# Layer A, pairs 1 to 6: the products of probabilities with values in one piece, begun later behind the border of the half products

## The chip, the cores and the metric

One core of one Trainium2 chip runs the whole program. The metric is device time in microseconds (us), the median of the runs shown. Five engines work side by side, each through its own list of instructions in order: TensorE (PE), VectorE (DVE), ScalarE (ACT), GpSimd (POOL) and SyncE (SP, which here only issues transfers).

## What is computed

The reference is an encoder block of two layers over 512 tokens of width 1024, 16 heads of 64. Layer A is dilated attention in three groups that are merged by their denominators; layer B is attention over a neighbourhood on a grid. Cut to layer A, where the change is:

```python
def mixer_a(hn, w_in, w_out, q_gain, k_gain, t5_bias):
    proj = hn @ w_in
    ...
    for g, (window, dilation) in enumerate(DILATED_PAIRS):
        q = rms_norm(qkv[:, :, g, 0], q_gain[g])
        k = rms_norm(qkv[:, :, g, 1], k_gain[g])
        v = qkv[:, :, g, 2]
        ...
    alpha = jax.nn.softmax(jnp.stack(lses), axis=0)
    y = jnp.sum(alpha[..., None] * jnp.stack(outs), axis=0)
    y = y.reshape(b, s, BRANCH_WIDTH).astype(hn.dtype) * jax.nn.silu(gate)
    return y @ w_out
```

## The kernel before, in words

**Precision.** Every float32 operand of a large product is split into a rounded part and a rest (`wh` and `wl` for weights, `hn_h` and `hn_l` for the normalised input), and a product is three matmuls of 512 columns into a bank of PSUM called `acc`. ACT makes `wh` from the loaded weights `wraw`, and DVE or POOL makes `wl`. `splits` hands out these weight tiles in the order of a plan, one tile of 512 columns being a job; there are 6 buffers for `wh`, 5 for `wl`, 8 for `wraw`.

**Layer A.** The 16 heads are worked in 8 pairs, 0 to 7, by `main_a(hc)`. From pair 1 on, the projections to q, k and v are made by seven half-size block products in Strassen's manner (`product`), 32 jobs a pair with the gate and the first value group. The point behind the product that ends the queries is stamped `border`; one half product (4 jobs, 24 matmuls) follows it, and then the next pair begins.

**Side work.** A second generator, `side`, does the attention of pair hc while `main` makes the projections of pair hc + 1. For each pair it runs `attn_a`: the scores in two halves (`scores`, tile `log`), softmax on DVE and ACT (`minima`, `exponents`, `normalise`), a turn of the probabilities `p` into `pt`, transfers `pt<-pt` on SP, the transpose of the values (`v_a`, tile `tp`), the products of probabilities with values (`weigh`, four banks `o`, tile 32*64 for groups 1 and 2 and 128*64 for group 0), the multiplication with the gate on DVE (`weighed`, `gt<-gt,o`), a send of `gt` to memory (`y_d<-gt`), and the transposes of the next pair's queries and keys (`q_a`, `k_a`, tiles `tp<-rawq` and `tp<-rawk`). Those read `rawq` and `rawk` after DVE has scaled them (`rawq<-rawq,rs`, `rawk<-rawk,rs`), the scale coming from a chain of nine small DVE operations that begins at `nv<-ss` (`unit`).

**What sets the order.** The order on PE is the order in which the program is written out. `run` steps `main` one group of matmuls at a time and lets `side` put in a piece when a clock that the program counts itself (`clock`, in ns of PE work as `matmul` estimates it) has reached the time that the piece asked for; a guard in `main` can force `side` on until a stamp is there. `later_on(delay, job)` puts small jobs of DVE and ACT into a list of timers, and `tick` runs those that are due. `weigh` yields twice, so that the 96 products of a pair come in three pieces: 32 for group 1, 32 for group 2, 32 for group 0, with the gaps that the caller names. The order on DVE, ACT, POOL and SP is set by a scheduler from dependencies and the order of issue, but for lines marked to stay in program order.

Of the kernel before, what the change touches and what calls it, by code (L numbers as in the profile page):

```python
# [26 lines left out]
NHC = 8  # L27
# [23 lines left out]
def tile_hybrid_encoder(  # L51
# [287 lines left out]
    clock = [0.0]  # L339
# [22 lines left out]
                hs = slice(64 * hd, 64 * hd + 64)  # L362
                matmul(os[hd], l(hs), r(hs), share=2, start=(n == 0), stop=(last and n == 2))

    timers = []

    def later_on(delay, job):

        timers.append((clock[0] + delay, job))
        timers.sort(key=lambda t: t[0])  # L370

    def tick(all_of=False):
        while timers and (all_of or timers[0][0] <= clock[0]):
            timers.pop(0)[1]()

    chores = []

# [267 lines left out]
    def part(n, cols=512):  # L645
        half = rk[:, 2048 * (n % 2) : 2048 * (n % 2) + 4 * cols]
        return half.rearrange("p (i c) -> p i c", i=4)

    def raw_q():
        return wk.tile([P, 4, 512], F32, tag="rawq", name="rawq", bufs=1)  # L650

    def sums():
        return wk.tile([P, 32], F32, tag="ss", name="ss", bufs=3)
# [75 lines left out]
    def main_a(hc):  # L729
        if hc == 0:  # L730
            yield from project_qk(512, 8, "rawq", hc, None, first=True, need="na")
            yield from project_qk(512, 4, "rawk", hc, ("rs", "a"), after=renorm)
            return

        kv, a, b, c, box = part(hc), [], [], [], [sums(), sums()]

        def new():
            if len(box) == 2:
                box.append(raw_q())
            return box[2]  # L740

        hn = lambda k0, t0: lambda k: (t[:, k0 + k, t0 : t0 + H] for t in (hn_h, hn_l))
        mixed = lambda n: lambda k: (t[:, n, k, :] for t in (mix_h, mix_l))

        def keep(i, acc):
            act.copy(kv[:, 2 + i, :], acc)

        def put11(i, acc):
            act.copy(kv[:, i, :], acc)
            squares_soon(kv[:, i, :256], box[0], i, 4)  # L750

        def put_v(i, acc):
            vec.tensor_sub(new()[:, 2 + i, :], acc, kv[:, 2 + i, :])

        def put_u(i, acc):
            vec.scalar_tensor_tensor(
                box[2][:, i, :], acc, -1.0, kv[:, 2 + i, :], op0=ALU.mult, op1=ALU.subtract
            )

        def put12(i, acc):  # L760
            t = box[2][:, i, :]
            vec.tensor_add(t, t, acc)
            squares_soon(t, box[1], i, 8)

        def put22(i, acc):
            t = box[2][:, 2 + i, :]
            vec.tensor_sub(t, t, acc)
            squares_soon(t, box[1], 2 + i, 8)

        def put21(i, acc):  # L770
            t = kv[:, 2 + i, :]
            vec.tensor_add(t, t, acc)
            squares_soon(t[:, :256], box[0], 2 + i, 4)

        yield from product(a, hn(0, 0), True, keep, ("w", hc - 2))
        yield from gate_a(hc - 1)
        yield from product(a, hn(KH, 0), False, put11)
        if hc > 1:
            yield from v0_a(hc - 1, ("scored", hc - 1))
        for n, acc, first, put in ((0, c, True, put_v), (1, b, True, put_u), (3, c, False, put12), (2, b, False, put22)):  # L780
            yield "mix", n
            yield from product(acc, mixed(n), first, put, ("q", hc - 1) if n == 0 else None)
        normed(box[2], box[1], 8, "rawq", hc)
        if hc == 1:
            yield from v0_a(hc - 1)
        stamp["border", hc] = clock[0]
        yield
        yield from product(b, hn(KH, H), False, put21)
        if hc == NHC - 1:
            st["y_h"] = big.tile([P, KT, S], F32R, tag="yh", name="y_h")  # L790
            st["y_l"] = big.tile([P, KT, S], F32R, tag="yl", name="y_l")
        normed(kv, box[0], 4, "rawk", hc)
        if hc == NHC - 1:
            yield ("back",)
            yield from v0_a(hc)
            yield from gate_a(hc)
# [57 lines left out]
                dl, src, gk[:, g : g + 1], dh.bitcast(F32), op0=ALU.mult, op1=ALU.subtract  # L854
            )

    def side_by_side(mms, outs=1, gaps=None):


        for i, (d, v, r) in enumerate(mms):  # L860
            if i and outs > 1 and i % 16 == 0:
                yield gaps[i // 16 - 1]
            for hd in range(2):
                hs = slice(64 * hd, 64 * hd + 64)
                matmul(d(hs), v(hs), r(hd), share=2 * outs if i < 32 and outs > 1 else 2,
                       start=i < outs, stop=i >= len(mms) - outs)
# [35 lines left out]
    def weighed(hc, os):  # L902
        gt, rest = st.pop(("gate", hc))
        for _ in rest:
            pass
        for j in range(4):
            g = by_class(gt)[:, :, j]
            vec.tensor_mul(g, g, os[j][:, :P].rearrange("p (t r) -> p t r", t=4))
        return gt
# [91 lines left out]
    def attn_a(hc):  # L1001
# [107 lines left out]
            dst = sb(pq, at(t, hd), [[256, 2], [1024, 4], [1, 32]])  # L1109
            vec.tensor_copy(dst, tp.rearrange("p (i a r) -> p i a r", i=2, a=4))  # L1110

        def weigh(first=2200):
            os, v0 = [bank("o") for _ in range(4)], st.pop("v0")
            mms = []
            for g in range(2):
                for b in range(4):
                    for j in range(4):
                        own = slice(32 * j, 32 * j + 32)
                        c, d = P * g, 1024 * b + 256 * (2 + g)
                        mms.append((  # L1120
                            lambda hs, j=j: os[j][hs, :P],
                            lambda hs, own=own, b=b, c=c: v12[own, b, c + hs.start : c + hs.stop],
                            lambda hd, own=own, d=d: pq[own, d + at(0, hd) : d + at(0, hd) + P],
                        ))
            for i in range(4):
                (ta, ia), (tb, ib) = ((i - 1, 1), (i, 0)) if i else ((0, 0), (3, 1))
                n, m = 32 * (tb - ta), 256 * (ib - ia) + 32 * (tb - ta)
                for a in range(4):
                    mms.append((
                        lambda hs, a=a, d=32 * ta, n=n: sb(os[a][hs], d, [[n, 2], [1, 32]]),  # L1130
                        lambda hs, i=i: v0[:, i, hs],
                        lambda hd, d=run * a + 256 * ia + 32 * ta, m=m: sb(t0[0], d + 128 * hd, [[m, 2], [1, 32]]),
                    ))
            yield from side_by_side(mms, 4, (first, 2200))
            return os

        if last:
# [16 lines left out]
            stamp["ya", "last", "p"] = 0  # L1154
            yield from v_a(hc)
            yield "wait", ("gate", hc), 500
            gt = weighed(hc, (yield from weigh()))
            held[0] = False
            stamp["ya", "turned"] = 0
            for c in range(4):  # L1160
# [26 lines left out]
        if hc:  # L1187
            st["e", hc + 1] = bias_a(hc + 1, True)
        if hc:
            yield "wait", ("border", hc + 1), 0  # L1190
        yield "wait", ("gate", hc), 4000
        gt = weighed(hc, (yield from weigh((2200, 6000)[hc] if hc < 2 else 4800 if hc == NHC - 2 else 3300)))
        if not hc:
            st["e", hc + 1] = bias_a(hc + 1)
        if hc < NHC - 2:
# [455 lines left out]
```

## Time and profile before

| | |
|---|---|
| median of 3 runs | 826.37 us (826.36 to 826.44) |
| the profiled execution | 827.79 us, its span 826.0 us |
| mean granted TensorE clock | 0.996 |
| busy: PE, DVE, ACT, POOL | 816.8, 608.3, 520.4, 236.2 us |
| products `o` of layer A, first and last | 117.4 us and 537.1 us into the span |

In the profile a line of the timeline has the start, the duration, the engine, the line of the program (L347 is the helper `matmul`, L351 `transpose`, L87 the wrapper that all other engines' operations go through), the operation, the tile written and the tiles read, the shape, and how many were merged. A bracket behind it has the time that the engine had stood idle, and who ended that. PE's matmuls are pipelined: the distance between starts says what a matmul costs, not its duration. A matmul on plain float32 operands leaves two records, so the 32 products of a group, `x32` in the order, are `x64` in the trace.

### The profile page before, as it was taken

How to read it: one execution, taken by the hardware profiler on the slowest of the kernel's cores; microseconds unless marked ns; L12 is line 12 of the kernel's file. 1: busy time of each engine (PE TensorE's matmuls, PEld its weight loads, DVE VectorE, ACT ScalarE, POOL GpSimd, SP SyncE). 2: the span in 40 equal slices, each digit the busy share in tenths (PEclk: the TensorE clock that was granted, in tenths of full speed). 3: DMA queues.
4: the chain of work that ended last, by engine and by line, in shares of the span. 5: the costliest groups of instructions: out<-in, count | busy, mean ns of one | idle time of the engine just before them, and what ended most of it. 6: DMA issues, size and time to landing. Idle time of an engine off the chain costs nothing.

```text
span 826.0 us, 17436 instructions
## 1 busy us (share of the span) xinstructions
PE 816.8 (99%) x6410; PEld 660.3 (80%) x6410; DVE 608.3 (74%) x1546; ACT 520.4 (63%) x1075; POOL 236.2 (29%) x194
## 2 busy tenths in 40 slices
PE   9999999999999999999999999999999999999998
PEld 7876788778778888888888888888888787888776
DVE  7897896797798777777777785547656769776453
ACT  8668665855755945946946947644567476766340
POOL 0042402442351531531531525412111122122220
PEclk9999899999999999999999999999999999999999
DMA  9426666576575784784774755384244563744122
GB/s 344 149 64 177 158 155 165 116 207 182 119 196 182 163 214 135 162 212 138 162 211 138 162 174 182 97 300 153 94 162 141 152 186 132 206 115 145 36 103 102
DMA packets 54869, 131.92 MB, mean 160 GB/s; under 512 B 6784, under 2 KB 24384, under 8 KB 54656
## 3 DMA queue, kind: packets, MB, share of 16 engines
q1 hardware_dynamic: 48304, 108.27, 41.5%
q0 software_dynamic: 6048, 22.02, 14.8%
q8 instruction: 50, 0.82, 0.4%
q10 hardware_dynamic: 432, 0.52, 0.2%
q14 instruction: 35, 0.29, 0.1%
HBM read 111.73 MB, written 11.72 MB: 149 GB/s over the span
## 4 chain that ended last, share of the span: by engine, by line
PE 94%; DVE 2%; ACT 2%; issue 1%; POOL 1%; DMA 0%; SPq 0%; DVEq 0%; ACTq 0%; POOLq 0%
PE acc L347 78%; PE o L347 6%; PE log L347 6%; PE tp L351 4%; POOL wl L87 1%; ACT wh L87 1%; DVE mixed L87 0%; DMA wraw<-in_w 0%; ACT rawk L87 0%; DVE wl L87 0%; PE pk L347 0%; DVE pt L87 0%; DVE ss L87 0%; DVE mix_l L87 0%; ACT k L87 0%
## 5 line engine op out<-in xcount | busy, mean ns | idle before, releaser
L87 ACT CAST wh<-wraw 128x512 fp32r<-128x512 f32 (+1 forms) x344 | 206.5, 611 | 142.8 <-PE acc L347 120.6
L87 POOL TENSOR_TENSOR wl<-wraw,wh 128x512 fp32r<-128x512 f32 (+1 forms) x126 | 172.5, 1384 | 415.3 <-PE acc L347 170.6
L87 DVE TENSOR_TENSOR wl<-wraw,wh 128x512 fp32r<-128x512 f32 (+1 forms) x218 | 166.9, 769 | 57.5 <-PE acc L347 36.6
L347 PE MATMUL acc<-wh,hn_h 128*128 128x512 f32 x424 | 172.2, 407 | 0.9 <-ACT wh L87 0.6
L347 PE MATMUL acc<-wl,hn_h 128*128 128x512 f32 x424 | 165.3, 391 | 0.4 <-DVE wl L87 0.4
L347 PE MATMUL acc<-wh,hn_l 128*128 128x512 f32 x424 | 165.2, 391 | 0.0
L87 ACT ACTIVATE p<-p,mn 128x256 f32<-128x256 f32 (+2 forms) x248 | 138.1, 582 | 29.9 <-DVE mn L87 29.8
L347 PEld LDWEIGHTS acc<-wh,hn_h 128*128 128x128 f32 x424 | 79.5, 188 | 21.1 <-issue 3.4
L347 PEld LDWEIGHTS acc<-wh,hn_l 128*128 128x128 f32 x424 | 79.6, 188 | 17.4
L347 PEld LDWEIGHTS acc<-wl,hn_h 128*128 128x128 f32 x424 | 79.8, 188 | 15.6 <-DVE wl L87 1.2
L347 PE MATMUL acc<-wh,mix_h 128*128 128x512 f32 x224 | 89.8, 401 | 0.0
L347 PE MATMUL acc<-wl,mix_h 128*128 128x512 f32 x224 | 88.5, 395 | 1.2 <-POOL wl L87 1.2
L347 PE MATMUL acc<-wh,mix_l 128*128 128x512 f32 x224 | 88.0, 393 | 0.0
L347 PE MATMUL acc<-hn_h,wh 128*128 128x512 f32 x192 | 78.5, 409 | 0.0
L347 PE MATMUL acc<-hn_l,wh 128*128 128x512 f32 x192 | 75.1, 391 | 0.0
L347 PE MATMUL acc<-hn_h,wl 128*128 128x512 f32 x192 | 75.0, 391 | 0.0
L87 POOL DMA_DIRECT2D wraw<-in_w x42 | 38.7, 936 | 81.7 <-DVE wl L87 74.2
L87 DVE TENSOR_REDUCE ss<-sq 128x8 f32<-128x512 f32 (+1 forms) x80 | 44.7, 573 | 21.8 <-ACT sq L87 20.9
L87 DVE STREAM_TRANSPOSE pt<-p 128x512 f32<-128x512 f32 (+1 forms) x60 | 40.4, 684 | 21.5 <-ACT p L87 21.5
L347 PE MATMUL acc<-y_h,wh 128*128 128x512 f32 x128 | 51.7, 404 | 0.0
L347 PEld LDWEIGHTS acc<-wl,mix_h 128*128 128x128 f32 x224 | 42.5, 190 | 11.2 <-POOL wl L87 2.0
L347 PEld LDWEIGHTS acc<-wh,mix_h 128*128 128x128 f32 x224 | 42.5, 190 | 10.2 <-issue 1.8
(152 smaller groups left out, 1332.8 us busy)
## 6 DMA issues: line engine op xcount, KB each, us to landing
wraw<-in_w SPq DMA_DIRECT2D x119, 512.0 KB
wraw<-in_w POOLq DMA_DIRECT2D x42, 512.0 KB, 7.4
pt<-pt SPq DMA_DIRECT2D x106, 64.0 KB
td<-tr SPq DMA_DIRECT2D x24, 224.0 KB
pt<-td SPq DMA_DIRECT2D x24, 224.0 KB
e<-l_d SPq DMA_DIRECT2D x32, 112.0 KB
wraw<-in_w SPq DMA_DIRECT2D x6, 384.0 KB
e<-l_d SPq DMA_DIRECT2D x16, 128.0 KB
```

Source lines behind the costliest of these rows:

```text
L87: m = f(*args, **kw)
L347: nc.tensor.matmul(o, l, r, **kw)
L351: nc.tensor.transpose(o, i, ident)
```

## The change

The diff does four things. `weigh` takes both of its gaps from the caller, and a gap of 0 is no yield at all, so in pairs 1 to 6 the 96 products stand in one piece; pairs 0 and 7 keep their gaps of 2200. The wait on the border of the next pair asks for 2300 ns behind it (3800 in pair 6) where it asked for none. A job that a timer issues counts its own timers from the time at which it was due, and no longer from the time at which the list was looked at; this holds for every pair and for layer B. The second tile of sums of squares (`ss`) is taken when the queries' tile is taken, no longer at the pair's start.

```diff
-    timers = []
+    timers, due_at = [], [None]
 
     def later_on(delay, job):
 
-        timers.append((clock[0] + delay, job))
+        timers.append(((clock[0] if due_at[0] is None else due_at[0]) + delay, job))
         timers.sort(key=lambda t: t[0])
 
     def tick(all_of=False):
         while timers and (all_of or timers[0][0] <= clock[0]):
-            timers.pop(0)[1]()
+            due_at[0], job = timers.pop(0)
+            job()
+            due_at[0] = None
...
-        kv, a, b, c, box = part(hc), [], [], [], [sums(), sums()]
+        kv, a, b, c, box = part(hc), [], [], [], [sums()]
 
         def new():
-            if len(box) == 2:
-                box.append(raw_q())
+            if len(box) == 1:
+                box.extend((sums(), raw_q()))
             return box[2]
...
-    def side_by_side(mms, outs=1, gaps=None):
+    def side_by_side(mms, outs=1, gaps=(0, 0)):
 
         for i, (d, v, r) in enumerate(mms):
-            if i and outs > 1 and i % 16 == 0:
+            if i and outs > 1 and i % 16 == 0 and gaps[i // 16 - 1]:
                 yield gaps[i // 16 - 1]
...
-        def weigh(first=2200):
+        def weigh(gaps):
...
-            yield from side_by_side(mms, 4, (first, 2200))
+            yield from side_by_side(mms, 4, gaps)
...
-            gt = weighed(hc, (yield from weigh()))
+            gt = weighed(hc, (yield from weigh((2200, 2200))))
...
         if hc:
-            yield "wait", ("border", hc + 1), 0
+            yield "wait", ("border", hc + 1), 3800 if hc == NHC - 2 else 2300
         yield "wait", ("gate", hc), 4000
-        gt = weighed(hc, (yield from weigh((2200, 6000)[hc] if hc < 2 else 4800 if hc == NHC - 2 else 3300)))
+        gt = weighed(hc, (yield from weigh((0, 0) if hc else (2200, 2200))))
```

The order of instructions shows what moves. On PE, pair 1, the first piece of products stood right at the border, behind the last matmuls on `mix_h` and `mix_l` (the operands of the half products ahead of the border):

```order
L347 MATMUL acc<-wh,mix_h 128x512
L347 MATMUL acc<-wl,mix_h 128x512
L347 MATMUL acc<-wh,mix_l 128x512
L347 MATMUL o<-pt,rawk 64x128 x32
L347 MATMUL acc<-wh,hn_h 128x512
L347 MATMUL acc<-wl,hn_h 128x512
L347 MATMUL acc<-wh,hn_l 128x512
```

In the changed kernel it stands 12 matmuls behind the border, with all three groups in it:

```order
L347 MATMUL acc<-wh,hn_h 128x512
L347 MATMUL acc<-wl,hn_h 128x512
L347 MATMUL acc<-wh,hn_l 128x512
L347 MATMUL o<-pt,rawk 64x128 x64
L347 MATMUL o<-pt_1932,v_1945 64x2x32 x8
L347 MATMUL o<-pt_1932,v_1945 64x64 x24
L347 MATMUL acc<-wh,hn_h 128x512
L347 MATMUL acc<-wl,hn_h 128x512
L347 MATMUL acc<-wh,hn_l 128x512
```

The other two pieces of before are gone from their places, 30 and 12 matmuls further on (18 and 12 in pairs 2 to 5; in pair 6, 24 and none). Behind the piece the first transposes of the next queries come after 30 matmuls (24 in pair 6), where they came 15 behind the third piece (18 in pair 6).

On DVE, pair 3, the next pair's queries were scaled ahead of the multiplication with the gate:

```order
L87 TENSOR_TENSOR rawq<-rawq,rs 128x512
L87 TENSOR_TENSOR wl<-wraw,wh 128x512
L87 TENSOR_TENSOR rawq<-rawq,rs 128x512
L87 TENSOR_TENSOR wl<-wraw,wh 128x512
L87 TENSOR_TENSOR rawk<-rawk,acc 128x512
L87 TENSOR_TENSOR rawq<-rawq,rs 128x512
L87 TENSOR_TENSOR rawk<-rawk,acc 128x512
L87 TENSOR_TENSOR rawq<-rawq,rs 128x512
L87 TENSOR_TENSOR wl<-wraw,wh 128x512
L87 TENSOR_TENSOR gt<-gt,o 128x4x32 x4
```

Now the multiplication, which reads what the piece writes, stands ahead of them, right behind the chain of small operations that gives `rs`:

```order
L87 SCALAR_TENSOR_TENSOR rs<-na,rs 128x32
L87 TENSOR_TENSOR gt<-gt,o 128x4x32 x4
L87 TENSOR_TENSOR rawq<-rawq,rs 128x512 x2
L87 TENSOR_TENSOR wl<-wraw,wh 128x512
L87 TENSOR_TENSOR rawq<-rawq,rs 128x512
L87 TENSOR_TENSOR wl<-wraw,wh 128x512
L87 TENSOR_TENSOR rawk<-rawk,acc 128x512
L87 TENSOR_TENSOR rawq<-rawq,rs 128x512
L87 TENSOR_TENSOR rawk<-rawk,acc 128x512
L87 TENSOR_TENSOR wl<-wraw,wh 128x512
```

So the four scalings of `rawq` changed places with the multiplication, and in DVE's order all that follows, weight rests `wl` among it, stands behind what reads the piece's result.

On ACT, in pair 0, some 60 us into the program, the keys of pair 0 are scaled in sixteen small operations, and `mix_h` is rounded, whose input DVE makes:

```order
L87 ACTIVATE rawk<-rawk,rs 128x64 x4
L87 CAST wh<-wraw 128x512
L87 CAST mix_h<-mixed 128x1024
L87 ACTIVATE rawk<-rawk,rs 128x64 x8
L87 CAST wh<-wraw 128x512
L87 ACTIVATE rawk<-rawk,rs 128x64 x4
L87 ACTIVATE gt<-acc 128x512
```

The timers now count from due times, and the second group of four stands ahead of `mix_h`:

```order
L87 ACTIVATE rawk<-rawk,rs 128x64 x4
L87 CAST wh<-wraw 128x512
L87 ACTIVATE rawk<-rawk,rs 128x64 x4
L87 CAST mix_h<-mixed 128x1024
L87 ACTIVATE rawk<-rawk,rs 128x64 x8
L87 CAST wh<-wraw 128x512
L87 ACTIVATE gt<-acc 128x512
```

One group of four moved from behind the second `wh` to ahead of `mix_h`. On SP the send `y_d<-gt` now stands one load of weights earlier, right behind the bias loads of the next pair; POOL's list is the same in layer A up to two rows in pair 7.

## Prediction

> **What bounds the kernel now.** I read the page first, then who PE waited for, then PE's timeline around the pieces, and last DVE and ACT where the order changes.
>
> ```profile
> PE 816.8 (99%) x6410; PEld 660.3 (80%) x6410; DVE 608.3 (74%) x1546; ACT 520.4 (63%) x1075; POOL 236.2 (29%) x194
> ```
>
> PE is busy for 816.8 of 826.0 us, so only PE's own time and its few waits can be shortened. The longest of those waits:
>
> ```profile
> PE log L347 <- ACT k L87: 1.6, 2, 0.8
> PE acc L347 <- POOL wl L87: 1.2, 2, 0.6
> ```
>
> Each row has the sum in us, the number of times and the longest; the rows left out are smaller or lie ahead of the first product. A gain must come from what the pieces cost PE, from the two waits for POOL, from the two for ACT's `k`, or from the clock.
>
> **Part 1: the seams.** PE's timeline in pair 2, at the three pieces, with the last matmul ahead and the first two behind each:
>
> ```profile
> 235.43 0.39 PE L347 MATMUL acc<-wh,mix_l 128*128 128x512 f32 x1
> 235.75 1.21 PE L347 MATMUL o<-pt,rawk 32*64 32x128 f32 x64
> 236.89 0.50 PE L347 MATMUL acc<-wh,hn_h 128*128 128x512 f32 x1
> 237.22 0.40 PE L347 MATMUL acc<-wl,hn_h 128*128 128x512 f32 x1
> ...
> 240.87 0.39 PE L347 MATMUL acc<-wh,hn_l 128*128 128x512 f32 x1
> ...
> 242.33 0.50 PE L347 MATMUL acc<-wh,hn_h 128*128 128x512 f32 x1
> ...
> 244.95 0.39 PE L347 MATMUL acc<-wh,hn_l 128*128 128x512 f32 x1
> ...
> 247.28 0.50 PE L347 MATMUL acc<-wh,hn_h 128*128 128x512 f32 x1
> 247.62 0.39 PE L347 MATMUL acc<-wl,hn_h 128*128 128x512 f32 x1
> ```
>
> And two places where pieces already stand together, pair 0 (its second and third) and pair 7 (all three):
>
> ```profile
> 121.14 0.39 PE L347 MATMUL acc<-wh,hn_l 128*128 128x512 f32 x1
> 121.46 1.21 PE L347 MATMUL o<-pt,rawk 32*64 32x128 f32 x64
> 122.60 2.08 PE L347 MATMUL o<-pt,v 128*64 128x64 f32 x64
> 124.61 0.50 PE L347 MATMUL acc<-wh,hn_h 128*128 128x512 f32 x1
> ...
> 532.64 0.39 PE L347 MATMUL acc<-y_l,wh 128*128 128x512 f32 x1
> 532.87 0.40 PE L347 MATMUL acc<-y_h,wl 128*128 128x512 f32 x1
> 533.19 2.10 PE L347 MATMUL o<-pt,rawk 32*64 32x128 f32 x128
> 535.22 2.09 PE L347 MATMUL o<-pt,v 128*64 128x64 f32 x64
> 537.34 0.50 PE L347 MATMUL acc<-y_h,wh 128*128 128x512 f32 x1
> 537.68 0.40 PE L347 MATMUL acc<-y_l,wh 128*128 128x512 f32 x1
> ```
>
> Undisturbed matmuls start 0.23 us apart (532.64 to 532.87). A piece costs PE the distance from the last `acc` ahead to the first behind, less 0.23, and 0.10 more, since the next matmul then starts 0.33 and not 0.23 later. First piece: 236.89 - 235.43 - 0.23 + 0.10 = 1.33. Second: 242.33 - 240.87 gives the same 1.33. Third: 247.28 - 244.95 - 0.23 + 0.11 = 2.21. Together 4.87 us a pair.
>
> In one piece there are two ends. Pair 7 has it whole: 537.34 - 532.87 - 0.23 + 0.11 = 4.35, a saving of 0.52. Or pair 0's joined pieces, 124.61 - 121.14 - 0.23 + 0.11 = 3.35, and the other 64 records by pair 7's longer run, (535.22 - 533.19) - (122.60 - 121.46) = 0.89: 4.24, a saving of 0.63. I take 0.63, because pair 0 is followed by ordinary products as pairs 1 to 6 are, while pair 7's goes on into a fresh bank. Pairs 1 to 5 lose both seams: 5 x 0.63 = 3.15. In pair 6 the second and third pieces already touch in the order, so it goes from 1.33 + 3.35 = 4.68 to 4.24 and saves 0.44. Sum 3.6 us; with 0.52 instead, 5 x 0.52 + 0.33 = 2.9.
>
> Most of the saving lies at the first seam (0.44 of 0.63): from group 2 to group 0 the tile changes from 32*64 to 128*64, and that costs PE nearly the same with or without other work between. The Trainium skill, "TensorEngine Tiling (Array Packing)", section Key Properties, says that a change of tiling mode drains the engine. Three pieces have six such changes and one has three; were all six alike, the saving would be larger at the second seam than the rows allow, so the sum goes by the rows.
>
> **Part 2: pair 2's late weights.** PE's wait for POOL in the middle of the mixed products, and POOL's own row:
>
> ```profile
> 226.62 0.40 PE L347 MATMUL acc<-wh,mix_h 128*128 128x512 f32 x1
> 227.59 0.50 PE L347 MATMUL acc<-wl,mix_h 128*128 128x512 f32 x1 [0.57 <-POOL wl L87]
> ...
> 226.25 10.15 POOL L87 TENSOR_TENSOR wl<-wraw,wh 128x512 fp32r<-128x512 f32 x7 [3.00 <-ACT wh L87]
> ```
>
> POOL had stood idle for 3.00 us for a `wh` that ACT had queued behind softmax. It costs PE 227.59 - 226.62 - 0.23 + 0.10 = 0.84. The same wait is in pair 1 and in no later pair. In the order, the two halves of the scores are 21 matmuls apart in pairs 1 and 2 and 33 in pairs 3 to 6: with 21 the halves' softmax work piles up on ACT. In the changed order pair 1 still has 21, pairs 2 to 6 have 36, since `q_a` no longer comes behind a piece that waited 6000 ns in pair 1. So pair 2's 0.84 goes and pair 1's stays. Bounds: 0 (it is late anyway) and 1.7 (both go, ACT's exponents being issued earlier by the due times).
>
> **Part 3: pair 0, ACT.** The due times move four small scalings ahead of `mix_h`. ACT, then PE, then the granted clock:
>
> ```profile
> 63.53 1.07 ACT L87 ACTIVATE rawk<-rawk,rs 128x64 f32<-128x64 f32 x4 [2.06 <-DVE rs L87]
> ...
> 66.41 1.05 ACT L87 CAST mix_h<-mixed 128x1024 fp32r<-128x1024 f32 x1 [1.29 <-DVE mixed L87]
> ...
> 69.79 1.06 ACT L87 ACTIVATE rawk<-rawk,rs 128x64 f32<-128x64 f32 x4
> ...
> 79.37 0.38 PE L347 MATMUL log<-k0h,q0h 64*128 64x256 f32 x1 [0.84 <-ACT k L87]
> 80.47 0.58 PE L347 MATMUL log<-k0h,q0h 64*128 64x256 f32 x1 [0.72 <-ACT k L87]
> ```
>
> ACT idles 1.29 us ahead of `mix_h` and is then busy without a break until it has written `k`, for which PE waits twice; four scalings of 1.06 fit into the idle time. The group of four that stood at 69.79 is then done, and ACT reaches `k` about 1.0 us earlier. The first wait of 0.84 goes, the second stays (two `k` follow each other on ACT with a `wh` between), and so 0.84 to 1.1 is saved. I take 1.0; the bounds are -0.5 (a group of `wl` is now later behind sums of squares on DVE) and 1.6 (both waits).
>
> **Part 4: what could be late next.** DVE, in order, now holds the multiplication with the gate ahead of the scaling of `rawq`, so the scalings, `wl` and everything else queue up until the piece ends. The rows for the length of that queue, pair 2:
>
> ```profile
> 247.28 0.87 DVE L87 TENSOR_TENSOR gt<-gt,o 128x128 f32<-128x128 f32 x4
> 248.07 0.73 DVE L87 TENSOR_REDUCE ss<-sq 128x4 f32<-128x256 f32 x2
> 248.72 0.68 DVE L87 TENSOR_TENSOR wl<-wraw,wh 128x512 fp32r<-128x512 f32 x1
> 249.32 0.16 DVE L87 TENSOR_SCALAR nv<-ss 128x16 f32<-128x16 f32 x1
> ...
> 251.20 0.43 DVE L87 TENSOR_TENSOR rawk<-rawk,rs 128x256 f32<-128x256 f32 x1
> ...
> 250.82 0.60 PE L351 MATMUL tp<-ident,rawq 128*128 128x128 f32 x4
> ...
> 259.53 0.60 PE L351 MATMUL tp<-ident,rawk 128*128 128x128 f32 x4
> ```
>
> Count from the piece's end. The multiplication takes 0.8; an operation of 512 columns takes 0.60 of DVE (248.72 to 249.32). The fourth `rawq` is the seventh behind it: 0.8 + 7 x 0.60 = 5.0, say 5.3 with the landing. PE reaches the transposes of `rawq` after 30 matmuls, 30 x 0.23 = 6.9. Slack 1.6. The first `wl` (pair 3's job 2) is ready at 0.8 + 3 x 0.60 = 2.6; by the order the rests of four jobs of six matmuls stand ahead of it and last PE for 24 x 0.23 = 5.5, so 2.9 of slack. `rawk`: up to the next `wl` 6.2, two sums and one `wl` 1.3, the nine small operations 1.9 (249.32 to 251.20), then four scalings of about 0.4, three `wl` and one write of `k0l`: 4.0 more, 13.4 and with landings 14.5. Its transposes come 259.53 - 250.82 = 8.7 behind those of `rawq`: 6.9 + 8.7 = 15.6. Slack 1.1. In pair 2 three small operations for layer B's bias tables also stand ahead of it, which takes some of that. So I cost this at 0, with up to 0.5 in pair 2. The cover is DVE's speed: if it ran 2 us later, PE would wait 0.9 in each of five pairs.
>
> The send `y_d<-gt`, now one weight load earlier on SP, waits for a `gt` that is also ready earlier; the loads behind it wait for a free `wraw` buffer anyway: 0. POOL's list is unchanged here: 0. The second `ss` tile has three buffers and no wait in the trace: 0. Holding all four `o` banks takes 4.2 us in one piece instead of 11.9 (235.75 to 247.62), and the next transpose is 30 matmuls away: 0.
>
> **The sum.** 3.6 + 0.84 + 1.0 = 5.4 us off the profiled execution of 827.79 (span 826.0 and 1.8 around it, which the change doesn't touch), and so off the median of 826.37, which is 1.4 below that execution: 821.0 us.
>
> **The rivals.** *The clock stays up* (0.32).
>
> ```profile
> 80.00:84.00 4.00, 3.53 (x71) 0.53 0.95 167
> 84.00:88.00 4.00, 4.00 (x13) 0.62 1.05 202
> ```
>
> The 0.53 and 0.62 are the granted clock: right behind the two waits in pair 0 it was half for some 4 x 0.47 x 2 + 4 x 0.38 x 2 = 6.8 us, from about 80.24 on; PE waited up to 80.47, so 6.6 us of work were done at half clock, which cost 3.3. If the first wait goes, PE is idle for 0.7 and not 1.6 just before, and the clock may not fall: 5.4 + 3.3 = 8.7, 817.7 us. For it speaks that the waits of 0.57 and 0.60 for POOL lowered no clock: the mean of 0.996 over 826.0 us is a loss of 3.3, this one fall. Against it speaks that one wait is left. The Trainium skill, "TensorE: Matmul & The Clock Gate", Part 1, has the clock halve only after a whole idle window of about 3.4 us. The trace disagrees: it fell after waits of 0.84 and 0.72. By the rule this rival would have no cause at all.
>
> *Only the seams* (0.17). ACT in pair 0 gains nothing, POOL is late elsewhere, or one or two transposes wait: 2.4 to 3.6, 823.4 us. For it: parts 2 and 3 rest on order alone.
>
> *DVE held by the piece: slower* (0.06).
>
> ```profile
> 233.53 1.72 DVE L87 TENSOR_TENSOR wl<-wraw,wh 128x512 fp32r<-128x512 f32 x1
> ```
>
> This one took 1.72 while POOL was at work on its own `wl`. If three of the operations behind the multiplication do, each 1.12 longer than 0.60, the fourth `rawk` comes 3.4 later and PE waits 2.3 for it in each of five pairs, 11.5 against 5.4: 832.5 us. It decides from a lateness of 2.2 us on (1.1 of slack and 5.4 / 5). Against it: POOL has little work just there.
>
> *No change* (0.07). The waits of part 4 come to 0.7 in each of five pairs and pair 0 goes the wrong way by 0.5, with nothing from part 2: 3.6 - 3.5 - 0.5, 826.8 us.
>
> **How the numbers follow.** The forecast has 0.38. A measurement of this kernel tells 0.2%, 1.7 us, from no change. The range leaves out the last two rivals and a little on either side: low 817.2 (the clock stays up, and half of pair 1's wait goes too), high 824.2 (seams at 2.9 and some waits). Faster by over 0.2%: the forecast, the clock, and nearly all of the seams' case, 0.86; within: 0.08; slower: 0.06.
>
> **What would show it.** Right: in pairs 1 to 6 one run of `o` records with about 4.5 us from the last `acc` ahead to the first behind; no wait for POOL near 226 us; the first `log` wait in pair 0 gone; no wait of `tp` for `rawq` or `rawk`. Wrong: a row "PE tp <- DVE rawk" or "<- DVE rawq" of a us or more, new waits for `wl` behind the pieces, or a piece that costs as much as the three did. The clock at 80 to 87 us tells the forecast from the first rival.

## The result, and the profile after

The changed kernel takes 834.97 us (median of 5, 832.99 to 837.96) where the kernel before took 826.37: a ratio of 1.011, 95% interval 1.0086 to 1.0135. It is slower by 8.6 us; the forecast was 5.4 us faster. The profiled execution of after took 837.96 us with a span of 836.2, against 827.79 and 826.0.

From the page: PE's busy time, the queue on which PE's instructions come, and the shares of the chain that ended last.

```profile
PE 816.6 (98%) x6410; PEld 662.0 (79%) x6410; DVE 608.2 (73%) x1546; ACT 516.8 (62%) x1075; POOL 234.9 (28%) x194
...
q8 instruction: 50, 0.82, 0.4%
...
PE 86%; DVE 6%; ACT 4%; issue 3%; DMA 0%; DVEq 0%; SPq 0%; ACTq 0%
```

PE is as busy as before, but in a longer span, so the new time is waiting. The chain, which had 1% of "issue" before, has 3%. Who PE waited for (sum, times, longest):

```profile
PE o L347 <- issue: 9.8, 4, 4.1
PE acc L347 <- DVE wl L87: 1.5, 3, 1.0
...
PE log L347 <- ACT k L87: 1.2, 2, 0.7
PE acc L347 <- DVE rawq L87: 1.2, 6, 0.2
```

The first row is nearly the whole loss: four waits inside the products `o` for which the profile names no engine and no transfer. PE's timeline in pairs 1, 2 and 4 shows where they stand:

```profile
173.66 2.10 PE L347 MATMUL o<-pt,rawk 32*64 32x128 f32 x128
175.69 1.50 PE L347 MATMUL o<-pt,v 128*64 128x64 f32 x44
180.38 1.33 PE L347 MATMUL o<-pt,v 128*64 128x64 f32 x20 [3.19 <-issue]
...
241.27 2.09 PE L347 MATMUL o<-pt,rawk 32*64 32x128 f32 x128
243.30 2.08 PE L347 MATMUL o<-pt,v 128*64 128x64 f32 x64
...
365.80 2.14 PE L347 MATMUL o<-pt,rawk 32*64 32x128 f32 x128
367.87 1.84 PE L347 MATMUL o<-pt,v 128*64 128x64 f32 x55
373.80 0.55 PE L347 MATMUL o<-pt,v 128*64 128x64 f32 x9 [4.09 <-issue]
374.28 0.80 PE L347 MATMUL acc<-wh,hn_h 128*128 128x512 f32 x1
```

In pair 2 the piece runs through: 4.36 us from the start of the last `acc` ahead to the start of the first one behind. In pair 1 PE stops with 20 of group 0's 64 matmul records to go, in pair 4 with 9. By the same distance the pieces of pairs 1 to 6 take 8.30, 4.36, 5.89, 8.80, 4.36 and 5.90: the stalls are 3.9, 0, 1.5, 4.4, 0 and 1.5, together 11.4 us. (From one start to the next at the stop itself they are 3.4, 1.4, 4.3 and 1.5; the rest of the two long ones is products at the lowered clock that follows.)

**What the stalls have in common.** A record here is any instruction of PE in the trace: 12,820 matmuls and weight loads and 128 others, nearly all on semaphores, 12,948 in all. Counted so, PE stops at the records 2752, 5056, 6336 and 8640, to within one. Each of them leaves the remainder 192 when divided by 256. The queue "instruction" has 50 packets of 0.82 MB together, 16 KB each, and 50 times 256 is 12,800. A packet is then a block of 256 records. The trace has the start and the landing of a packet, but not the request for it. In no trace of this study does a packet start more than 298 records before PE needs it; with some 1.2 us between request and start, 309 records is my estimate of the notice. At the pace of the half products (about 8.8 records per us) that is 35 us. In the one piece, which passes some 386 records in 4.3 us, it is about 3.5 us, and the packet took longer. The queues of the transfers from 371.4 to 372.6 us (packets, MB, share) have one packet of it; from 366.0 to 371.4 there was none, and PE had stood still since 369.5:

```profile
q8 instruction: 1, 0.02, 5.1%
```

PE goes on at 373.80, 1.4 us behind the landing at 372.41. In the 17 stalls at a block's end, in all traces of this study, PE goes on 1.2 to 1.7 us behind the landing of the queue's packet. Where a request falls against the piece decides: 1187 records a pair are 4.64 blocks, so the place shifts from pair to pair. The requests in the table are estimates, put 309 records ahead; with 298 they come up to 1.6 us later.

| pair | request (estimate), records behind the piece's beginning | runs dry at (+309; the piece has 386) | request (estimate), us | landed, us | stall, us |
|---|---|---|---|---|---|
| 1 | 38 | 347 | 173.87 | 178.91 | 3.9 |
| 2 | 131 | 440, behind the piece | 242.21 | 249.20 | 0 |
| 3 | -32 | 277 | 298.56 | 304.86 | 1.5 |
| 4 | 61 | 370 | 366.21 | 372.41 | 4.4 |
| 5 | 154 | 463, behind the piece | 434.24 | 440.09 | 0 |
| 6 | -21 | 288 | 493.40 | 498.66 | 1.5 |

The Trainium skill, "Runtime: NRT & Kernel Launch", "Instruction fetch mechanics", says that instructions are refilled in blocks of 16 KiB or 256 instructions by the engine's own DMA queue. The trace agrees, 50 packets for 12,948 records. The same section says that this is hidden because an engine dispatches more slowly than it is filled; at the 60 to 140 records per us of these products the trace disagrees, with stalls of up to 4.4 us.

**The clock** fell behind the two long stalls. Windows of pair 4; the columns behind the busy times of PE, PEld, DVE, ACT and POOL are the granted clock, the share of DMA and GB/s:

```profile
366.00:370.00 4.00, 3.71 (x183) 3.41 (x173) 1.96 (x10) 0.58 (x1) 0.64 (x1) 1.00 0.91 237
370.00:374.00 4.00, 0.20 (x7) 0.20 (x8) 0.00 (x0) 0.00 (x0) 0.00 (x0) 1.00 0.85 208
374.00:377.40 3.40, 3.40 (x16) 2.65 (x12) 3.35 (x8) 0.11 (x1) 0.00 (x0) 0.50 0.51 160
377.40:380.00 2.60, 2.60 (x13) 2.10 (x12) 2.25 (x5) 1.45 (x3) 0.86 (x1) 1.00 0.92 229
```

The window at 0.50 stands behind the stall of 4.4 us. Pair 1 has a longer one, from 179.4 to 186.3 us, from within its stall of 3.9 on; the stalls of 1.5 us lowered nothing.

**Smaller differences.** PE's rows with a wait in pair 0 (the first three) and at the border of pair 2:

```profile
77.99 0.38 PE L347 MATMUL log<-k0h,q0h 64*128 64x256 f32 x1 [0.44 <-ACT k L87]
...
110.97 0.50 PE L347 MATMUL acc<-wl,hn_h 128*128 128x512 f32 x1 [0.97 <-DVE wl L87]
...
113.38 0.50 PE L347 MATMUL acc<-wl,hn_h 128*128 128x512 f32 x1 [0.30 <-DVE wl L87]
...
238.33 0.47 PE L347 MATMUL acc<-wh,hn_h 128*128 128x512 f32 x1 [0.19 <-DVE rawq L87]
```

In pair 0 the first wait for `k` is 0.44 instead of 0.84, and the clock stays up at 80 to 88 us (1.00, where it was 0.57 in the mean), but PE, now earlier, meets DVE and waits for `wl` at 111 and 113 us, which costs it about 1.7. At each border the first matmul, which adds to a bank that DVE has just read (`rawq<-rawq,acc`), now comes 0.58 behind the one ahead of it where 0.23 is the pace. Before, the first piece of products stood in that gap. In pair 1 the wait for POOL (0.60 at 164.90 before) has become a smaller one for DVE:

```profile
160.59 0.50 PE L347 MATMUL acc<-wl,mix_h 128*128 128x512 f32 x1 [0.24 <-DVE wl L87]
```

**The account**, up to the first product of pair 7 (533.19 before, 543.26 after, +10.1): pair 0 -2.6; stalls +11.4; the clock behind them about +3.4 (2.0 and 1.4, what is left of those two pairs); the border +2.5 (0.35 and a slower matmul behind it, 0.08, six times); seams -3.6; the wait for POOL in pair 2 -0.8; -0.3 is left, about what pair 1's wait lost (the matmul came 1.00 behind the one ahead of it and now comes 0.63 behind).

### The profile page after: what moved, and what is told of

It reads as the page before. It is cut to its first block, busy times and chain, and to the rows that moved or that the text cites. A ratio compares the mean times of both kernels' runs of the same rounds, so it can differ in the third digit from the quotient of the medians.

```text
span 836.2 us, 17391 instructions
## 1 busy us (share of the span) xinstructions
PE 816.6 (98%) x6410; PEld 662.0 (79%) x6410; DVE 608.2 (73%) x1546; ACT 516.8 (62%) x1075; POOL 234.9 (28%) x194
## 4 chain that ended last, share of the span: by engine, by line
PE 86%; DVE 6%; ACT 4%; issue 3%; DMA 0%; DVEq 0%; SPq 0%; ACTq 0%
PE acc L347 71%; PE o L347 6%; PE log L347 5%; PE tp L351 4%; DVE wl L87 1%; ACT p L87 1%; DVE rawq L87 1%; ACT wh L87 1%; ACT rawk L87 1%; DVE p L87 1%; DVE mixed L87 1%; DVE pt L87 1%; DMA wraw<-in_w 0%; DVE ss L87 0%; ACT y_h L87 0%
## 5 line engine op out<-in xcount | busy, mean ns | idle before, releaser
L87 DVE TENSOR_TENSOR wl<-wraw,wh 128x512 fp32r<-128x512 f32 (+1 forms) x218 | 160.2, 738 | 55.6 <-PE acc L347 29.6
L347 PE MATMUL acc<-wl,hn_h 128*128 128x512 f32 x424 | 167.0, 395 | 1.3 <-DVE wl L87 1.3
L347 PE MATMUL acc<-y_h,wl 128*128 128x512 f32 x128 | 50.1, 391 | 0.0
L347 PE MATMUL acc<-y_l,wh 128*128 128x512 f32 x128 | 50.0, 390 | 0.0
```

Source lines behind the costliest of these rows:

```text
L87: m = f(*args, **kw)
L347: nc.tensor.matmul(o, l, r, **kw)
```

## The experiments

Three theories. **Supply**: PE runs out of instructions in the dense piece. **Data**: the piece waits for something that it reads. **DVE and border**: the stalls are by the way, and the later border and the order on DVE make the loss. "Before" in the numbers is the kernel before on the same chip; in the jobs of several rounds its median was 826.38 (the first four) and 826.47 (the next four).

### Move the count, leave the work

```diff
     for _ in range(8):
         nc.tensor.matmul(busy, ones[:, :P], ones, start=True, stop=True)
+    for _ in range(48):
+        nc.tensor.matmul(busy[:, :32], ones[:, :P], ones[:, :32], start=True, stop=True)
```

> The changed kernel with 48 tiny matmuls (128x32) more among the warm-up matmuls at the start, 96 records of PE ahead of everything else; all later work is the same. The first theory (supply) says that PE runs out of instructions inside the one piece: its instructions come in blocks of 256 (50 transfers of 16 KB on the queue named instruction, 12,820 records), the trace of the changed kernel shows each block asked for about record 256*i+140 and PE standing still at record 256*i+448, so the place of the piece in the count decides. 96 records more move that place by 96 in every pair: the request, which came 38, 131, -32, 61, 154 and -21 records behind the piece's beginning in pairs 1 to 6, comes at -58, 35, -128, -35, 58 and -117. Expected: no stall (under 0.3 us) in pairs 1, 3 and 6, 3 to 4 us in pair 2, about 4 us in pair 5, 1 to 2 us in pair 4, each at 309 records behind the request; time 831 to 836. The second theory (data) says that the piece waits for something that it reads, the transfers of pt or the values: the stalls stay in pairs 1, 3, 4 and 6 with 3.4, 1.4, 4.3 and 1.5 us and pairs 2 and 5 stay free; time 834 to 836. The third (DVE and border) says that the stalls are by the way and that the loss is made by the wait at the border and by the order on DVE: 834 to 836, wherever the stalls are.

Measured: 844.09 us (839.25 to 846.78). The stalls moved as supply said. PE's timeline in pairs 1, 2, 4 and 5:

```profile
181.22 2.17 PE L347 MATMUL o<-pt,rawk 32*64 32x128 f32 x128
183.33 2.08 PE L347 MATMUL o<-pt,v 128*64 128x64 f32 x64
...
244.86 1.50 PE L347 MATMUL o<-pt,v 128*64 128x64 f32 x42
250.12 1.11 PE L347 MATMUL o<-pt,v 128*64 128x64 f32 x22 [3.77 <-issue]
...
375.14 1.86 PE L347 MATMUL o<-pt,v 128*64 128x64 f32 x56 [1.17 <-issue]
...
441.92 0.90 PE L347 MATMUL o<-pt,v 128*64 128x64 f32 x10 [3.57 <-issue]
```

Pairs 1, 3 and 6 have none (4.44, 4.43 and 4.37 us from `acc` to `acc`), pair 2 has 4.3, pair 4 1.5 and pair 5 4.3. That speaks against data, which has no reason to move; the dense run below settles it. The total missed supply's 831 to 836: I had not priced the 48 matmuls, 0.15 us each, which put off the first product from 5.65 to 12.02 us. Without those 6.4 us it is 837.7. Another 1.4 us went right behind them, where the granted clock was at half up to 15.0 us: the matmul that starts at 8.48 us in after starts at 16.23 here. That leaves 836.3.

### Three pieces again, the rest kept

```diff
-        gt = weighed(hc, (yield from weigh((0, 0) if hc else (2200, 2200))))
+        gt = weighed(hc, (yield from weigh(((2200, 6000)[hc] if hc < 2 else 4800 if hc == NHC - 2 else 3300, 2200))))
```

> The changed kernel with the three pieces and the gaps of before (the joining undone, the later border, the due times and the later ss kept). Supply: three pieces of 128 records with 2 to 7 us between them let the next block land, so no stall in any pair; pair 0's gain at its products (2.6 us) and the new wait of PE for DVE's rawq at the border (0.35 to 0.43 in six pairs, 2.1 to 2.6) about cancel, the seams are those of before: 826.2, range 824.5 to 827.5. Data: the group that waited stands 5 us later, so no stall either, 826.2. DVE and border: the loss stays, 831 to 835.

Measured: 832.08 us (831.97 to 834.32), ratio 1.0076 (1.0059 to 1.0094). No stall in any piece, as supply said, and yet 5.7 us slower than before, as the third theory said. Who PE waited for:

```profile
PE acc L347 <- DVE wl L87: 1.7, 7, 0.3
...
PE acc L347 <- DVE rawq L87: 1.2, 6, 0.2
```

One round, from the first `o` of pair 2 to that of pair 3, takes 63.23 us (237.11 to 300.34), against 61.73 in the kernel before (235.75 to 297.48). Beside the border's 0.43 about 1.0 is lost at the products of `mix_h`, at 285 to 289 us:

```profile
287.26 0.51 PE L347 MATMUL acc<-wl,mix_h 128*128 128x512 f32 x1 [0.23 <-DVE wl L87]
```

That is the place, one pair on, where the kernel before waited for POOL's `wl` in pair 2. That the three pieces, begun later, push the next pair's softmax into ACT's conversions there fits, but was not tried. So the third theory holds for three pieces begun later; it can't be the cause of after, which has none of these waits in pairs 2 to 6.

### The due times alone, and with the later `ss`

Both start from the kernel before; the second has the part on `box` as well.

```diff
-        timers.append((clock[0] + delay, job))
+        timers.append(((clock[0] if due_at[0] is None else due_at[0]) + delay, job))
...
-            timers.pop(0)[1]()
+            due_at[0], job = timers.pop(0)
+            job()
+            due_at[0] = None
...
-        kv, a, b, c, box = part(hc), [], [], [], [sums(), sums()]
+        kv, a, b, c, box = part(hc), [], [], [], [sums()]
...
-                box.append(raw_q())
+                box.extend((sums(), raw_q()))
```

> The kernel before with one part of the change alone: jobs of timers count their own timers from the time at which they were due. Supply and data alike: pair 0 keeps its granted clock up at 80 us, its first wait of log for ACT's k goes, part is lost again to waits for wl at 109 to 113 us; the products of pair 0 begin at 114.8 instead of 117.4, and as nothing else is changed this 2.6 us stays to the end: 823.8, range 822 to 826. DVE and border: later pairs give it back, 826 or more.

> The kernel before with the due times and the later taking of the second tile of sums of squares, pieces, gaps and border as before. The due times alone gave 1.1 us (the products of pair 0 begin at 116.5 instead of 117.4), the runs with both begin them at 114.8 to 115.4. Supply and data: the later ss is worth the other 1.2 to 1.5 us in pair 0 and nothing later: 824.0, range 823 to 825.3. If the ss tile does nothing, 825.3.

Measured: 825.28 us, ratio 0.9989 (0.9976 to 1.0001), and 825.39 us, ratio 0.9991 (0.9979 to 1.0002). Both missed the middle by some 1.4 us; the second lies just outside its range, where it was expected if the `ss` tile does nothing. Together with `ss` the products of pair 0 begin at 115.32 in the profile instead of 116.53, but these 1.2 us are there long before: PE's early wait for `rawk` ends at 53.02 us in the one and at 54.21 in the other, and from there to the products it is 62.3 us in both, as in after. The first record of the granted clock begins at 7.3 us in the one and at 9.5 in the other. The lowest execution is the same, 824.8, with and without these parts and in the kernel before; what differs is how many lie near it: 8 of 12 and 7 of 11 executions are below 825.5, and of the kernel before 7 of 23 and 5 of 29. So the gain in pair 0 is about 1 us in the median, not 2.6, and both intervals reach 1. The due times also changed both of PE's waits for POOL into the smaller ones for DVE; in pair 2 of the first:

```profile
225.04 0.50 PE L347 MATMUL acc<-wl,mix_h 128*128 128x512 f32 x1 [0.23 <-DVE wl L87]
```

### Two pieces

```diff
-        gt = weighed(hc, (yield from weigh((0, 0) if hc else (2200, 2200))))
+        gt = weighed(hc, (yield from weigh((0, 4800) if hc else (2200, 2200))))
```

> The changed kernel with the products in two pieces in pairs 1 to 6: groups 1 and 2 together (256 records), group 0 (128) 4800 ns behind them. Supply: a request at or behind the beginning of the first piece has 309 records to go, of which the first piece has at most 256 and the gap some 40 at the slow pace, so the block has 7 us or more to land: no stall, or under 0.5 us in one pair. One seam of two is saved (0.44 us in six pairs, 2.6), the border costs 2.1 to 2.6 and pair 0 gains 2.6: 823.6, range 822 to 826. Data: the same, since group 0 stands 4.8 us later. DVE and border: 830 to 834.

Measured: 824.55 us (824.24 to 827.03), ratio 0.9985 (0.9974 to 0.9996), with no stall in any pair and the waits at the border still there. Who PE waited for, and the two pieces of pair 4, where the one piece had its longest stall:

```profile
PE acc L347 <- DVE rawq L87: 1.2, 6, 0.2
```

```profile
359.50 2.12 PE L347 MATMUL o<-pt,rawk 32*64 32x128 f32 x128
...
367.21 2.08 PE L347 MATMUL o<-pt,v 128*64 128x64 f32 x64
```

A gap of 4.8 us asked for between 256 and 128 records turns 834.97 into 824.55. The round takes 61.71 us (236.09 to 297.80), as with the gaps and the border of before: the seam saved, 0.44, pays for the border, 0.43.

### One piece right at the border

```diff
-            yield "wait", ("border", hc + 1), 3800 if hc == NHC - 2 else 2300
+            yield "wait", ("border", hc + 1), 0
```

> The changed kernel with the one piece begun right at the border (the wait of 2300 and 3800 set back to 0). Supply: the piece stands some 24 records of PE earlier in the count (40 in pair 6), so the request for the next block comes 63, 154, -10, 82, 174 and 10 records behind its beginning in pairs 1 to 6, and PE runs dry 309 records behind the request if the block needs the 7 to 8 us that it needed so far. Expected: stalls of some 4 us in pair 1, 3 in pair 3, 3.5 in pair 4 (at 391, just behind the piece's own 386 records), 3.5 in pair 6, none in pairs 2 and 5; the wait for rawq at the border gone again, -2.4; about 14 us of stalls in place of 10.7: 835, range 832 to 838. Data: the piece stands 2.3 us earlier, so what it waits for is waited for longer: 5.5, 0 to 1, 3.5, 6.5, 0 to 1, 5.3. DVE and border: the border was the loss, so 828 to 832.5.

Measured: 832.53 us (830.62 to 841.4), ratio 1.01 (1.0063 to 1.0136). The waits for `rawq` are gone. PE's rows with a wait in pairs 1, 3, 4 and 6:

```profile
173.89 0.34 PE L347 MATMUL o<-pt,v 128*64 128x64 f32 x4 [1.24 <-DMA pt<-pt]
175.08 2.02 PE L347 MATMUL o<-pt,v 128*64 128x64 f32 x60 [0.85 <-DMA pt<-pt]
...
298.82 1.50 PE L347 MATMUL o<-pt,v 128*64 128x64 f32 x43 [0.50 <-issue]
...
363.50 0.40 PE L347 MATMUL acc<-wh,hn_l 128*128 128x512 f32 x1 [1.44 <-issue]
...
487.35 2.18 PE L347 MATMUL o<-pt,v 128*64 128x64 f32 x34 [3.21 <-issue]
```

Supply had the places right: none in pairs 2 and 5, and in pair 4 the stop comes behind the piece, at record 393 from its beginning where 391 was expected. The lengths it had wrong: 0.8, 1.4 and 4.5 us instead of 3, 3.5 and 3.5, and none in pair 1, since the blocks landed 2.6 to 5.1 us behind the request (its time estimated as above), where those that stalled PE in after took 5.0 to 6.3. And data has a share here: at the border group 0 really waits for the transfers of `pt`, 2.1 us in pair 1, at no block's end.

### Two pieces at the border, and one or two

```diff
-            yield "wait", ("border", hc + 1), 3800 if hc == NHC - 2 else 2300
+            yield "wait", ("border", hc + 1), 0
...
-        gt = weighed(hc, (yield from weigh((0, 0) if hc else (2200, 2200))))
+        gt = weighed(hc, (yield from weigh((0, 4800) if hc else (2200, 2200))))
```

> Two pieces as in the run with two pieces (gap 4800), but the first right at the border. Supply: no stall in any pair, since the piece of 256 records, some 40 at the slow pace and part of the last 128 leave the block 7 us or more; the wait for rawq at the border goes, 0.40 in six pairs, part comes back as the waits for wl of pairs 1 and 2 (0.6 each): 822.4, range 821 to 824.5. Data: the first piece stood without a wait 2.3 us later, so nothing is known against it at the border, 822.4 as well. DVE and border: if the early piece holds the queries' scaling on DVE as it did in the kernel before, 824 to 826.

The second kernel has one piece in pairs 2 and 5, `(0, 0) if hc in (2, 5) else (0, 4800)`.

> Right at the border, one piece in pairs 2 and 5 alone, two pieces (gap 4800) in pairs 1, 3, 4 and 6. Supply: the request comes 154 and 174 records behind the beginning in pairs 2 and 5, its limit 309 further lies some 80 records behind the piece, at 8.8 records per us, so no stall there: 0.44 less than two pieces in each of two pairs, 0.8 below the run with two pieces at the border: 821.6, range 820 to 824. Data: pairs 2 and 5 had no stall with one piece 2.3 us later, 0 to 1 us now: 822 to 824. DVE and border: no gain over two pieces.

Measured: 823.33 us (822.83 to 825.82), ratio 0.9968 (0.9959 to 0.9977), and 826.03 us (823.54 to 828.84), ratio 0.9991 (0.9977 to 1.0004). The first is the fastest kernel of this study, 3.1 us ahead of before. Its page, and its pieces in pair 2:

```profile
PE 811.8 (99%) x6410; PEld 658.8 (80%) x6410; DVE 607.8 (74%) x1546; ACT 521.3 (63%) x1075; POOL 235.0 (29%) x194
```

```profile
232.46 2.11 PE L347 MATMUL o<-pt,rawk 32*64 32x128 f32 x128
...
240.16 2.08 PE L347 MATMUL o<-pt,v 128*64 128x64 f32 x64
```

Its round takes 61.23 us (232.46 to 293.69), 0.5 less than before. The second kernel missed: its single pieces take 4.97 and 4.92 us, 0.6 above the 4.36 of after, with a stop behind 8 of group 0's matmul records:

```profile
237.31 1.86 PE L347 MATMUL o<-pt,v 128*64 128x64 f32 x56 [0.34 <-issue]
...
421.68 1.85 PE L347 MATMUL o<-pt,v 128*64 128x64 f32 x56 [0.26 <-DMA pt<-pt]
```

The place is no block's end; the second row names the transfers of `pt`. So at the border one piece can be too early for group 0, by 0.6 us here and 2.1 in pair 1 of the run before, and the second gap has a use of its own. The medians of the two kernels differ by 2.7 us and their lowest executions by 0.7, about what the pieces account for; the profiled execution of the second was already 1.5 us behind that of the first at 54.66 us, before pair 0's scores.

### A dense run of 1280 records

```diff
+            if hc == 5:
+                mms = mms[:16] * 8 + mms[16:]
```

> The changed kernel with the 32 products of group 1 issued eight times in a row in pair 5, a pair that had no stall (the sum holds them eight times, so the values of pair 5 are others). The piece has 384 + 896 = 1280 records, and nothing else is changed ahead of it. Supply: PE runs dry 309 records behind the request that comes 154 records behind the beginning, at 463, and from there every 256 records, at 719, 975 and 1231, whatever it reads; the first stall some 5 us (309 records at 138 per us are 2.3 us of the 7 to 8 that a block needs), the later ones 1 to 2 each, as the next request is then already out; if only one request is out at a time, 5 each. Data: the products repeated read what has been read, so no stall, and the piece takes its 4.24 + 7 times 0.93 us. The stalls of pairs 1 to 4 as in the changed kernel; in pair 6 the place in the count moves by 896 records, three and a half blocks, so its stall goes under supply and stays under data.

Measured: 846.65 us (one execution). PE's timeline in pair 5, and the instruction queue from the page:

```profile
426.27 3.67 PE L347 MATMUL o<-pt,rawk 32*64 32x128 f32 x232
434.53 5.73 PE L347 MATMUL o<-pt,rawk 32*64 32x128 f32 x256 [4.59 <-issue]
441.44 1.58 PE L347 MATMUL o<-pt,rawk 32*64 32x128 f32 x88 [1.18 <-issue]
442.95 1.38 PE L347 MATMUL o<-pt,v 128*64 128x64 f32 x38
445.38 1.03 PE L347 MATMUL o<-pt,v 128*64 128x64 f32 x26 [1.05 <-issue]
...
q8 instruction: 54, 0.88, 0.4%
```

PE stops 464, 720, 976 and 1232 records behind the piece's beginning, within one of what supply said, for 4.9, 0.5, 1.5 and 1.3 us (start to start). The rows on `rawk` behind the first stops read again what PE has already read, so no datum can be late there. The 896 records more are 3.5 blocks, and the queue has 4 packets more. In pair 6 the stall is gone (4.40 us from `acc` to `acc`), in pair 7, which had none, there is one of 0.9. In pairs 1 and 4 the stalls are 2.6 and 3.1, and in pair 3, against both expectations, there is none (4.39): by the packets' landings its block came at 300.97 us, before PE needed it.

The later stops of the long piece are shorter, but not because a request was out already. The next block's packet starts 1.1 to 1.3 us behind PE's going on and lands 1.9 to 2.4 us behind it. What had changed is the load of the transfers; that it makes the difference fits, but was not tried by itself. The windows, with the granted clock, the share of DMA and GB/s at the end:

```profile
430.00:434.50 4.50, 0.00 (x0) 0.00 (x0) 0.00 (x0) 0.00 (x0) 0.00 (x0) 1.00 1.02 252
434.50:438.00 3.50, 3.40 (x131) 3.00 (x131) 0.00 (x0) 0.00 (x0) 0.00 (x0) 0.57 0.29 103
438.00:442.00 4.00, 2.82 (x167) 2.58 (x172) 0.00 (x0) 0.00 (x0) 0.00 (x0) 0.95 0.20 68
```

The first block, asked for with the transfers at a share of about 1, landed some 5.9 us behind its estimated request.

### Both kernels once more

Nothing is edited.

> The kernel before once more, for its clock. The executions of the kernel before lie at about 824.9, 826.4, 827.0 and 829.6 us; the one profiled had the granted clock down at 80.3 to 87.1 us, which cost about 2.9 us. If the clock makes these groups, an execution at 824.9 shows no drop (clock 1.000) and begins the products of pair 0 at about 114.5, one at 826 to 827 a drop of one window or two. If not, the drop is there at any time.

> The changed kernel once more. Supply: the places of the stalls are fixed by the count of records, 2752, 5056, 6336 and 8640, in pairs 1, 3, 4 and 6; their lengths hang on when the transfer of the block lands and differ by up to 2 us from the first trace, and the clock's drops behind them differ too: 832.5 to 838. Data: places and lengths as before.

Measured: 827.59 us, with the clock down at 80 to 88 us again (0.57 in the mean, as in the first trace) and no wait of `o`; and 836.67 us, with the stalls at the same four records, 3.8, 1.4, 4.1 and 1.8 us long, and the clock down behind the first and the third. What decides the clock at 80 us is open. The kernel before had it down for 6.8 us in both traces that there are, but not in every execution: of its 29 in the job with the runs at the border, 14 have a mean granted clock of 1.000, 13 of 0.998 (one window of 3.4 us would be that) and 2 of 0.995, and those at 1.000 lie between 824.9 and 827.3 us, so the clock alone doesn't make the groups. Of the eleven traces with the due times, whose waits for `k` are 0.44 and 0.72 alike, seven have it at 1.00 there and four (three pieces, two pieces, one or two, the dense run) have it down for 3.4 us. That costs little: from the matmul that waits for `rawk` at 52 to 60 us to the first product of pair 0 it is 62.3 us in the seven and 62.8 in the four, which don't have the wait of 1.0 for `wl`; in the kernel before it is 64.8.

## Why the prediction was wrong

**The step that failed** is the end of part 4, "Holding all four `o` banks takes 4.2 us in one piece instead of 11.9 ... 0", and with it the argument in part 1, which took the joined pieces of pairs 0 and 7 as a sign that joining only saves. The piece was costed by its matmuls, its operands and its banks, and not by PE's own instructions, whose queue stood on the page with a share of 0.4%. Those of pairs 0 and 7 stall in neither kernel because of where they lie: pair 0's has 256 records, and pair 7's request, by the estimate, falls at 182 and 188, too late in the piece. Measured, the step cost 11.4 us of stalls and about 3.4 of clock. That the stops follow the count of records is shown: they moved when 96 records were put ahead, vanished with a gap of 4.8 us, and came every 256 records in a piece that read nothing new. None of the four rivals had this mechanism; the slower one came near the time (832.5) for a reason that the trace of after doesn't show.

**Part 1, the seams**, was right where there was no stall. Counted as the prediction counted, 4.36 from `acc` to `acc` less 0.23 and 0.10 more, the piece costs 4.23 us; 4.24 was forecast. So the 3.6 us were there, and the runs with two pieces, which keep most of them, show it.

**A cover missed.** The prediction named no cover for the first matmul behind the border. The first piece had hidden that matmul's wait for DVE's `rawq`; with the piece later, it costs 2.5 us of the 3.6 that the seams save.

**Part 2** was right for pair 2, where the wait for POOL at 227.59 is gone, and wrong for pair 1, whose wait didn't stay: 0.24 for DVE in place of 0.60 for POOL. The due times alone did that in both pairs (the matmul came 0.97 and 1.00 behind the one ahead of it, and 0.63 in that run). So they took 0.34 of pair 2's 0.84, and the distance between the scores' halves, to which the prediction put it (with the due times as a bound), at most the rest.

**Part 3 and the clock.** The first wait for `k` shrank by 0.40 and didn't go; 0.84 to 1.1 was forecast. The rival "the clock stays up" came true in the profile of after (0.32 was its chance), but 1.7 us of it went back to waits for `wl`, and in the medians of the two runs with these parts alone about 1.1 us is left. The 3.3 us of that rival were a loss of the profiled execution, and not of all: of the 52 executions of the kernel before in the jobs of several rounds, 24 have a mean granted clock of 1.000, so the median had less to gain.

**Part 4 otherwise** was right: no wait of `tp` for `rawq` or `rawk` appeared in after.

**The sign that the prediction named**, one run of `o` records with about 4.5 us, was the right one: 4.36 in two pairs, 5.9 to 8.8 in the other four.

## What to carry to other kernels

When small matmuls are put closer together, count their records (matmul and weight load, twice for plain float32) against the instruction queue: in this kernel 256 records a block, some 300 records of notice, and an estimated 2 to 10 us from request to landing. A run of 256 records with slower work behind it stayed free here, and one of 384 was a matter of where the block's end fell, so that any edit ahead of it moves the stalls to other places. When a piece is moved away from a place, ask which wait it covered there; here the one wait that the piece had hidden was worth 2.5 of the 3.6 us that the seams saved.

## What the runs showed of the hardware

- PE stood still for up to 4.9 us for its own instructions; the wait is put down to "issue", in which the profile shows nothing that PE waited for. In the run that went on, with the transfers at a share of 0.2 to 0.3, each 256 records more cost a stall of 0.5 to 1.5 us.
- The blocks travel among the other transfers: counted from the estimated request, the same block needed 6.2, 5.7 and 4.9 us in three executions (pair 4, record 6336), with stalls of 4.4, 4.1 and 3.1.
- The granted clock fell to half behind stalls of 3.9 and 4.4 us (after), 4.3 and 4.3 (the shifted count), 4.5 (one piece at the border) and 4.9 (the dense run), not behind those of 3.1 or less; in pair 0 of the kernel before it fell behind waits of 0.84 and 0.72, and behind 0.44 and 0.72 in four of eleven traces.
